# Weight casts in the recurrence hops of a bidirectional RWKV-7 layer: queued behind one kind of copy only

## The chip, the cores and the metric

The kernel runs on one core of a Trainium2 chip. The core has five engines, each with its own queue of instructions, which in the profile it works through in the order of the program: TensorE (PE, with a separate row PEld for its weight loads), VectorE (DVE), ScalarE (ACT), GpSimd (POOL) and SyncE (SP, which here only starts DMA transfers). The metric is the device time of one execution in microseconds, lower is better.

## The reference

The reference computes one layer of a diffusion backbone on 640 tokens: 128 context tokens and 512 latent tokens. Each token goes through a modulated norm and a wide projection; that feeds a bidirectional RWKV-7 recurrence (8 heads of width 64), an attention branch, two sigmoid gates, an output projection and a feed-forward block. All weights are float32. What matters here is the recurrence, run once forward and once backward per head:

```python
def _wkv_step(s, inp):
    r, w, k, v, a, b = inp
    sa = jnp.einsum("bhvk,bhk->bhv", s, a)
    s = s * w[:, :, None, :] + sa[..., None] * b[:, :, None, :] + v[..., None] * k[:, :, None, :]
    return s, jnp.einsum("bhvk,bhk->bhv", s, r)
...
s_f, y_f = _wkv_scan(s0[:, 0], rh, _heads(decay[:, :, 0]), _heads(k_dir[:, :, 0]), vh,
                     -kk, kk * _heads(iclr[:, :, 0]), False)
s_b, y_b = _wkv_scan(s0[:, 1], rh, _heads(decay[:, :, 1]), _heads(k_dir[:, :, 1]), vh,
                     -kk, kk * _heads(iclr[:, :, 1]), True)
...
merged = (jax.nn.sigmoid(gate_rw) * (o_rw @ p["w_o_rwkv"])
          + jax.nn.sigmoid(gate_na) * (o_na @ p["w_o_na"]))
```

## The kernel before

**Products in three parts.** Every float32 matrix is split into a rounded part `hi` and a rest `lo`, and a product is three matmuls: hi by hi, hi by lo, lo by hi. For a weight tile of 128x1024 that lies in `wst`, `wcast` (L184) makes the two parts. In the form that the stretch here mostly uses, ScalarE does two passes over the tile: `wlo = -wst` (L190) and `whi = wst` rounded (L192), and a DMA that POOL starts (L191) adds `wst` into the negated tile. In the other form ScalarE does the pass L192 alone and VectorE subtracts (L195).

**The recurrence in chunks of 64 tokens.** The 8 heads are taken as four pairs, `ct` = 0 to 3. For each pair the program goes through `main` (builds the triangular matrices `Nt` from `AG`, L1189), `inv` (inverts them on VectorE, gives `Rt`), and `carry` (L1371 on), which walks through eight hops `s` = 0 to 7. A hop serves both directions and both heads at once. In the profile a hop is this ring of small operations:

- PE multiplies `AG` by the state `ZV` (L1393), ScalarE copies the result to `x` (L1396). In the list of instructions the tile is `x`, its name in the code is `x0`.
- PE multiplies `Rt` by `x` (L1420), ScalarE copies these products into `ZV` (L1426).
- PE multiplies `TG` by `ZV` (L1433, and L1450 for the output), VectorE multiplies by the decay into the next state in `ZV` (L1445).

The hop after it can't start before L1445. At the end of `carry` ScalarE copies the output out (L1455).

**What fills the ring.** `carry` is a generator that stops three times in each hop: behind the copy to `x`, behind the copies into `ZV`, and behind the decays. At each stop `weave` (L1588) reads one entry of a table `plan` and queues other work: first so many matmuls from `fill` (the large projections, L223), then, by the entry's last digit, preparation of the next head pair through `beside` (L520): digit 1 stands for the second stretch (behind the copies into `ZV`), digit 2 for the third (behind the decays). The first stretch gets fill alone. `beside` queues items until a budget is spent, `bud=((1.8, 0.8), (1.3, 1.8))`: microseconds of ScalarE and of VectorE that the author gave to the second and to the third stretch. Each item states its own cost as such a pair.

**Two sources of items.** `beside` looks first at `pend`, work that the fill left for later (a copy of a finished projection out of PSUM, its token shift `u_out` and `shift` at L545 to L554, its activation L573, the cast of the next weight tile), and takes the head of that list if it is due. Otherwise it takes the next item of the generator `pg`. For `ct` 0 to 2 that is `prep` for the next head pair: norms and LoRA products (L645 to L684), decays (L693 to L707), the keys `NK` (L721 on ScalarE, L723 and L728 on VectorE), the tiles `BK` (L738, L742), `bv` (L747, L751). For `ct` = 3 it is `gate_a`, VectorE's gating of the merged attention output (L1579). What is left of `pg` in hop 7 is drained there by `last` (before the copies into `ZV` for `ct` 0 and 1, behind them for `ct` 2 and 3), and then VectorE makes the next pair's `AG` (L1168), which the next `main` needs. `NK` is a tile with a single buffer: the second direction's `NK` may be written only when L738, L742 and L747 have read the first one.

**The cast's place.** `stream` (L805 on) runs the projections unit by unit and, an eighth into each, leaves the cast of the next unit's weight tile in `pend`, due at once. Inside `carry` (`hold`) an item that is late by less than 24 fill matmuls isn't forced out, so `beside` decides where it goes. PE, POOL, DVE and ACT take this part of the program in exactly the order in which it is written (`manual_schedule(engines=FIRST)`).

## Time and profile before

| what | value |
|---|---|
| median of 3 runs | 1151.08 us (1150.06 to 1152.26) |
| the profiled execution, its own time | 1151.04 us |
| its span in the profile | 1149.3 us |
| TensorE busy in the span | 1117.0 us, 97% |
| ScalarE, VectorE, GpSimd busy | 533.7, 777.8, 195.1 us |
| granted TensorE clock | 0.995 of full speed |
| cast passes L190 and L192 | 1.02 to 1.07 us each for 128x1024 |

The times in the profile are in microseconds from the start of the span. The four `carry` stretches lie at about 298 to 342, 394 to 437, 492 to 536 and 598 to 630 us. In a row of the timeline stand: start, time from the first start to the last end, engine, line, operation, result and operand, shapes, count, and in brackets how long the engine sat idle before and who released it. Matmul rows overlap each other, so a PE row that starts where the row ahead ends is a PE that doesn't wait.

### The profile page before, as it was taken

The page shows a single profiled execution, that of the slowest core. Times are in us where ns is not written, and L with a number is a line of the kernel's source. Part 1 is how long each engine was busy: PE and PEld are TensorE (multiplying, and loading weights), DVE is VectorE, ACT ScalarE, POOL GpSimd, SP SyncE. Part 2 cuts the span into 40 slices and gives each one's busy share as a digit, 9 for nine tenths or more (in the row PEclk, how much of TensorE's full clock was granted, in tenths as well). Part 3 has the DMA queues.
Part 4 walks back from the last instruction along what each step waited for, and adds up shares of the span by engine and source line. Part 5 has one row for each costly group of instructions (what it writes and reads, how often), then busy time and mean ns, then how long its engine had stood idle before and what let it go on. Part 6 is the DMA issues. An engine that isn't in the chain of part 4 may idle for free.

```text
span 1149.3 us, 26860 instructions
## 1 busy us (share of the span) xinstructions
PE 1117.0 (97%) x11160; PEld 990.9 (86%) x11160; DVE 777.8 (68%) x1641; ACT 533.7 (46%) x1052; POOL 195.1 (17%) x262
## 2 busy tenths in 40 slices
PE   6999999999999999999999999999999999999998
PEld 4688878799888888888898788999899989998997
DVE  4565465769558847936787846897478747874775
ACT  4444576665465665456443524654134413441340
POOL 1163244321101212120100421110101010101000
PEclk8999999999999999999999999999999999999999
DMA  9752677654433533343743872222212221232122
GB/s 340 261 113 91 199 277 236 198 153 125 107 75 86 148 85 93 96 119 86 254 122 105 265 213 72 92 93 93 91 56 92 94 90 55 92 97 88 55 91 94
DMA packets 60482, 149.16 MB, mean 130 GB/s; under 512 B 7460, under 2 KB 22436, under 8 KB 60360
## 3 DMA queue, kind: packets, MB, share of 16 engines
q1 hardware_dynamic: 54888, 131.16, 34.7%
q0 software_dynamic: 4032, 14.68, 6.5%
q10 hardware_dynamic: 1440, 1.59, 0.5%
q8 instruction: 88, 1.44, 0.5%
q14 instruction: 34, 0.28, 0.1%
HBM read 118.41 MB, written 14.32 MB: 115 GB/s over the span
## 4 chain that ended last, share of the span: by engine, by line
PE 74%; DVE 10%; issue 8%; ACT 4%; DMA 2%; POOL 1%; SPq 0%; ACTq 0%; DVEq 0%; POOLq 0%
PE acc L311 24%; PE f L1856 21%; PE fl L223 8%; PE mm L223 5%; PE psa L1044 1%; PE lg L959 1%; PE pt L988 1%; DVE RL L1321 1%; DVE pr L1317 1%; PE po L1006 1%; PE w L1420 1%; PE w L1393 1%; DMA o<-o_d 1%; PE w L1433 1%; DMA wlo<-wst 1%
## 5 line engine op out<-in xcount | busy, mean ns | idle before, releaser
L1856 PE MATMUL f<-t,whi 128*128 128x320 f32 x640 | 141.7, 310 | 0.2
L311 PE MATMUL acc<-whi,u 128*128 128x512 f32 (+1 forms) x448 | 136.1, 386 | 0.0
L1856 PE MATMUL f<-b,whi 128*128 128x320 f32 x608 | 135.0, 310 | 0.4 <-DVE b L212 0.4
L223 PE MATMUL fl<-h,whi 128*128 128x320 f32 x672 | 121.4, 321 | 0.0
L1856 PEld LDWEIGHTS f<-t,whi 128*128 128x128 f32 x640 | 106.8, 188 | 0.8 <-issue 0.4
L223 PEld LDWEIGHTS fl<-h,whi 128*128 128x128 f32 x672 | 102.1, 189 | 4.6
L192 ACT CAST whi<-wst 128x1024 fp32r<-128x1024 f32 (+1 forms) x77 | 79.3, 1033 | 52.2 <-PE acc L311 41.5
L1856 PEld LDWEIGHTS f<-b,whi 128*128 128x128 f32 x608 | 101.7, 188 | 1.1 <-issue 0.6
L1856 PE MATMUL f<-t,wlo 128*128 128x320 f32 x320 | 98.9, 309 | 0.0
L311 PEld LDWEIGHTS acc<-whi,u 128*128 128x128 f32 x448 | 83.5, 188 | 16.6
L1856 PE MATMUL f<-b,wlo 128*128 128x320 f32 x304 | 94.1, 309 | 0.0
L1909 ACT CAST whi<-ws 128x1024 fp32r<-128x1024 f32 x40 | 42.0, 1051 | 104.5 <-PE f L1856 45.6
L311 PE MATMUL acc<-wlo,u 128*128 128x512 f32 (+1 forms) x224 | 86.3, 385 | 0.0
L1923 POOL TENSOR_TENSOR ws<-wst 128x512 f32<-128x512 f32 x20 | 29.1, 1454 | 334.7 <-DVE wlo L1912 226.3
L195 DVE TENSOR_TENSOR wlo<-wst,whi 128x1024 fp32r<-128x1024 f32 (+2 forms) x57 | 60.1, 1066 | 30.6 <-ACT whi L192 30.0
L311 PE MATMUL acc<-whi,h 128*128 128x512 f32 x240 | 79.2, 404 | 0.8 <-DVE h L436 0.8
L1724 DVE SCALAR_TENSOR_TENSOR tt<-acc,G 128x512 f32<-128x512 f32 (+1 forms) x51 | 34.7, 680 | 59.0 <-PE acc L311 45.4
L223 PE MATMUL fl<-h,wlo 128*128 128x320 f32 x336 | 63.8, 322 | 0.0
L1909 ACT CAST whi<-wst 128x1024 fp32r<-128x1024 f32 (+1 forms) x48 | 41.3, 869 | 42.3 <-PE acc L311 25.1
L1856 PEld LDWEIGHTS f<-t,wlo 128*128 128x128 f32 x320 | 60.1, 188 | 0.0
L1912 DVE TENSOR_TENSOR wlo<-ws,whi 128x1024 fp32r<-128x1024 f32 x40 | 55.4, 1386 | 5.4 <-ACT whi L1909 5.4
L1445 DVE TENSOR_TENSOR ZV<-w,Dt 64x128 f32<-64x128 f32 x64 | 18.4, 288 | 58.5 <-PE w L1433 57.4
(342 smaller groups left out, 2533.2 us busy)
## 6 DMA issues: line engine op xcount, KB each, us to landing
wst<-in_w_dram SPq DMA_DIRECT2D x66, 512.0 KB
wst<-in_w_rw_dram SPq DMA_DIRECT2D x31, 512.0 KB
wlo<-wst POOLq DMA_DIRECT2D x28, 512.0 KB, 4.7
wa<-in_w_ada_dram SPq DMA_DIRECT2D x24, 512.0 KB
f<-in_w_ada_dram SPq DMA_DIRECT2D x16, 512.0 KB
wst<-in_w_qkv_dram SPq DMA_DIRECT2D x12, 512.0 KB
o<-o_d SPq DMA_DIRECT2D x14, 320.0 KB
x<-in_xs_dram SPq DMA_DIRECT2D x8, 512.0 KB
```

The lines of the kernel that those rows point to most:

```text
L192: act.copy(hi[:, :n], st[:, :n])
L195: dve.tensor_tensor(out=lo[:, a:b], in0=st[:, a:b], in1=hi[:, a:b].bitcast(F32), op=ALU.subtract)
L223: pe.matmul(ps[:, :t1 - t0], w[:, a:a + 128], x[:, k0 + kt, t0:t1], start=n == 0, stop=n == 3 * nk - 1)
L311: pe.matmul(pss[i][:, a:b], lhs(x, kt, ts_), w[:, cs_], start=ki == 0 and n == 0, stop=ki == last and n == 2)
L959: pe.matmul(psl[:, hd, o_:o_ + n], qT[ft][rows, qs], x[rows, :], start=True, stop=True)
L988: pe.transpose(pst[:, c * 128:(c + 1) * 128], L[:, c * 128:(c + 1) * 128], ident)
L1445: dve.tensor_tensor(out=V(ZV[own, l + 1, h, :], [[128 * dl, 2], [1, 64]]), in0=V(pn[own, :], [[64, 2], [1, 64]], 64 * g), in1=V(Dt[own, 0, ...
L1724: dve.scalar_tensor_tensor(out=tt, in0=ps[:, a:b], scalar=c, in1=G[:, g, sl], op0=ALU.mult, op1=ALU.mult)
L1856: pe.matmul(ps[:, :H2], w_[:, c_], x_[:, kt, :], start=first and kt + n == 0, stop=last and kt == 3 and n == 2, skip_group_check=more)
L1909: act.copy(r[0][:, :width], src())
L1912: dve.tensor_tensor(out=r[1][:, :width], in0=src(), in1=r[0][:, :width].bitcast(F32), op=ALU.subtract)
L1923: eng_x(PRM["se"][i - 1]).tensor_tensor(out=o_, in0=x, in1=y, op=op)
```

## The change

Three edits. The cast's stated cost goes from 1.05 to 2.1 us of ScalarE. `beside` no longer takes the head of `pend` but looks through all due items: first those whose ScalarE cost is over 2 (only the casts), and these only if it was called for the second stretch (`wide`); then the others that are due. `weave` says which stretch it is.

```diff
-    def beside(gen, budget):
+    def beside(gen, budget, wide):
...
-            if pend and pend[0][0] <= 0:
-                _, c, fn = pend.pop(0)
+            due = [p for p in pend if p[0] <= 0]
+            due = [p for p in due if p[1][0] > 2 and wide] + [p for p in due if p[1][0] < 2]
+            if due:
+                _, c, fn = due[0]
+                pend[:] = [p for p in pend if p is not due[0]]
                 fn()
...
-                    later(lambda i=i: cast(i + 1), (1.05, 0), -off[0])
+                    later(lambda i=i: cast(i + 1), (2.1, 0), -off[0])
...
-                            beside(o_, bud[n - 1])
+                            beside(o_, bud[n - 1], n == 1)
```

In the second stretch's budget of 1.8 a cast now leaves no room for anything else; before, an item of `prep` followed it. No instruction is added or removed, but many of `prep` move to a later hop. Behind L526 the changed file's lines carry numbers that are 3 higher (L1429 there is L1426 before).

ScalarE, hops 6 and 7 of `ct` = 0, before. `x_682` and `x_688` are the two hops' copies to `x`; `U` and `vp` belong to a projection's token shift, `NK_4332` is the second direction's key tile:

```order
L1396 COPY x_682_4264<-w_4259 128x128
L1426 COPY ZV<-w_4275 64x2x64 x2
L545 COPY U_4057<-fl_4170 128x192
L546 COPY U_4057<-fl_4170 128x128
L551 ACTIVATE vp_627<-U_4057,D 128x128
L551 ACTIVATE vp_627<-U_4057,D 128x512
L190 ACTIVATE wlo_4313<-wst_4168 128x1024
L192 CAST whi_4312<-wst_4168 128x1024
L1396 COPY x_688_4322<-w_4317 128x128
L747 COPY bv_4329<-NK_4203 128x320 x2
L721 ACTIVATE NK_4332<-pre_4066,D 128x320 x2
L1426 COPY ZV<-w_4347 64x2x64 x2
```

The same place on ScalarE in the changed kernel:

```order
L1399 COPY x_681_4262<-w_4257 128x128
L1429 COPY ZV<-w_4273 64x2x64 x2
L190 ACTIVATE wlo_4288<-wst_4147 128x1024
L192 CAST whi_4287<-wst_4147 128x1024
L548 COPY U_4048<-fl_4149 128x192
L549 COPY U_4048<-fl_4149 128x128
L554 ACTIVATE vp_627<-U_4048,D 128x128
L554 ACTIVATE vp_627<-U_4048,D 128x512
L1399 COPY x_687_4320<-w_4315 128x128
L750 COPY bv_4329<-NK_4252 128x320 x2
L724 ACTIVATE NK_4332<-pre_4161,D 128x320 x2
L1429 COPY ZV<-w_4347 64x2x64 x2
```

The cast went from behind the token shift (third stretch) to directly behind hop 6's copies into `ZV`, and the token shift now stands behind it.

VectorE at `ct` = 0 from hop 5's decays on to the next pair's `AG`, before. `f_680` and `f_691` are the two directions' `BK`:

```order
L1445 TENSOR_TENSOR ZV<-w_4213,Dt_2031 64x2x64 x2
L728 TENSOR_TENSOR NK_4203<-NK_4203,kt__626 128x640
L738 SCALAR_TENSOR_TENSOR f_680_4257<-NK_4203,pre_3893 128x10x64
L552 SCALAR_TENSOR_TENSOR vp_627<-U_4057,C,vp_627 128x128
L554 SCALAR_TENSOR_TENSOR vp_627<-U_4057,C,vp_627 128x128
L1445 TENSOR_TENSOR ZV<-w_4266,Dt_2031 64x2x64 x2
L552 SCALAR_TENSOR_TENSOR vp_627<-U_4057,C,vp_627 128x512
L554 SCALAR_TENSOR_TENSOR vp_627<-U_4057,C,vp_627 128x512
L742 TENSOR_TENSOR f_680_4257<-NK_4203,pre_3893 128x10x64
L723 SCALAR_TENSOR_TENSOR NK_4332<-pre_4066,kk_4002 128x640
```

The same place on VectorE in the changed kernel:

```order
L1448 TENSOR_TENSOR ZV<-w_4203,Dt_2031 64x2x64 x2
L726 SCALAR_TENSOR_TENSOR NK_4252<-pre_3949,kk_4033 128x640
L731 TENSOR_TENSOR NK_4252<-NK_4252,kt__626 128x640
L1448 TENSOR_TENSOR ZV<-w_4264,Dt_2031 64x2x64 x2
L555 SCALAR_TENSOR_TENSOR vp_627<-U_4048,C,vp_627 128x128
L557 SCALAR_TENSOR_TENSOR vp_627<-U_4048,C,vp_627 128x128
L555 SCALAR_TENSOR_TENSOR vp_627<-U_4048,C,vp_627 128x512
L557 SCALAR_TENSOR_TENSOR vp_627<-U_4048,C,vp_627 128x512
L741 SCALAR_TENSOR_TENSOR f_688_4326<-NK_4252,pre_3948 128x10x64
L745 TENSOR_TENSOR f_688_4326<-NK_4252,pre_3948 128x10x64
L726 SCALAR_TENSOR_TENSOR NK_4332<-pre_4161,kk_4033 128x640
```

Three of these moved behind hop 6's decays: the two short token-shift passes and the first direction's L738 (now L741). From L723 of the second direction on to L1168 the order is the same in both.

VectorE in hop 5 of `ct` = 3, before. `mx_8653` gates a finished projection that lies in the PSUM tile `fl_8734`:

```order
L1579 SCALAR_TENSOR_TENSOR kk_8283<-pre_8655,kk_8283 128x320 x2
L1579 SCALAR_TENSOR_TENSOR bv_8420<-pre_8689,bv_8420 128x320 x2
L1554 SCALAR_TENSOR_TENSOR mx_8653<-mx_8653,fl_8734 128x320
L1556 TENSOR_TENSOR mt_7932<-mt_7932,mx_8653 128x320
L1445 TENSOR_TENSOR ZV<-w_8771,Dt_6879 64x2x64 x2
L195 TENSOR_TENSOR wlo_8813<-wst_8626,whi_8812 128x768
```

The same place in the changed kernel, where that tile is called `fl_8736`:

```order
L1582 SCALAR_TENSOR_TENSOR bv_8420<-pre_8659,bv_8420 128x320 x2
L195 TENSOR_TENSOR wlo_8794<-wst_8630,whi_8793 128x768
L1448 TENSOR_TENSOR ZV<-w_8771,Dt_6879 64x2x64 x2
L1557 SCALAR_TENSOR_TENSOR mx_8657<-mx_8657,fl_8736 128x320
L1559 TENSOR_TENSOR mt_7932<-mt_7932,mx_8657 128x320
```

The cast's VectorE half (L195) moved from behind hop 5's decays to ahead of them, and the gating that reads the PSUM tile moved from ahead of them to behind. In hop 2 of `ct` = 3, L195 stands directly ahead of the decays too.

## The prediction, made before the changed kernel ran

> **What bounds the kernel.** I read the page's first part, then the table of stretches, then the waits, then the timeline where the two orders differ. Page first:

> ```profile
> span 1149.3 us, 26860 instructions
> PE 1117.0 (97%) x11160; PEld 990.9 (86%) x11160; DVE 777.8 (68%) x1641; ACT 533.7 (46%) x1052; POOL 195.1 (17%) x262
> ```

> PE is busy for all but 32 us of the span: whatever makes it wait adds to the time, and little can be won. The table of stretches for the four `carry` stages (columns: start:end, us, then busy us and count of PE, PEld, DVE, ACT, POOL, the granted clock, the DMA share, GB/s):

> ```profile
> 298.00:342.00 44.00, 42.35 (x596) 36.61 (x595) 16.98 (x35) 27.50 (x71) 6.12 (x10) 1.00 0.33 82
> 394.00:437.00 43.00, 41.47 (x591) 35.91 (x591) 21.01 (x41) 26.62 (x71) 6.83 (x9) 1.00 0.31 85
> 492.00:536.00 44.00, 42.88 (x602) 37.55 (x602) 18.11 (x37) 26.62 (x72) 5.91 (x9) 1.00 0.37 98
> 598.00:636.00 38.00, 37.96 (x570) 32.81 (x570) 24.42 (x56) 13.52 (x40) 0.51 (x1) 1.00 0.41 125
> ```

> PE idles 1.65, 1.53, 1.12 and 0.04 us there, 4.3 us together: the ceiling of any gain. What ScalarE's queue costs PE at the copy to `x`, from the view of line L1396 ("who waited for it"), in all 32 hops:

> ```profile
>   PE w L1420: 1.6, 5
> ```

> So 1.6 us is what a cast, or something else ahead of that copy, costs now. The other side is what the cast pushes back.

> **The change, `ct` = 0.** The cast of hop 6 moves ahead of the token shift, `prep` runs one item or two later. The timeline of hops 6 and 7:

> ```profile
> 335.01 0.32 ACT L545 COPY U<-fl 128x192 f32<-128x192 f32 x1
> ...
> 335.53 1.02 ACT L551 ACTIVATE vp<-U,D 128x128 f32<-128x128 f32 x2
> ...
> 336.04 0.35 DVE L552 SCALAR_TENSOR_TENSOR vp<-U,C,vp 128x128 f32<-128x128 f32 x1 [1.94 <-ACT vp L551]
> ...
> 336.45 1.04 ACT L190 ACTIVATE wlo<-wst 128x1024 fp32r<-128x1024 f32 x1
> ...
> 337.40 1.03 ACT L192 CAST whi<-wst 128x1024 fp32r<-128x1024 f32 x1
> 337.54 0.75 DVE L552 SCALAR_TENSOR_TENSOR vp<-U,C,vp 128x512 f32<-128x512 f32 x1
> ...
> 338.99 0.82 DVE L742 TENSOR_TENSOR f<-NK,pre 128x640 f32<-128x640 f32 x1
> ...
> 341.31 0.73 PE L1450 MATMUL w<-TG,ZV 128*64 128x64 f32 x8 [0.71 <-ACT ZV L1426]
> ...
> 344.09 3.36 DVE L1168 TENSOR_TENSOR AG<-kk,P 64x640 f32<-64x640 f32 x4
> ...
> 347.50 1.27 PEld L1189 LDWEIGHTS w<-AG,f 64*32 64x32 f32 x122 [0.21 <-DVE AG L1168]
> ```

> The last row is what decides: the next `main` (L1189) waited for `AG`, so VectorE's tail of `prep` is already the end of the chain, with no slack. In the changed order that tail is longer. The two passes take 336.45 to 338.43, 1.98 us, and now lie ahead of L545, so the token shift's first VectorE pass starts 1.98 us after 336.04, at 338.0. Four shift passes follow (0.85 us from 336.04 to hop 6's decays at 336.89, and 1.45 us from 337.54 to 338.99): 340.3. Then L738 and L742, which both stand there now, 0.82 us each: 341.95. From the end of L742 to the end of L1168 the order is as before, 339.81 to 347.45, 7.64 us: `AG` is ready at 349.6 instead of 347.45, 2.1 us later. On the way, hop 7's copies into `ZV` stand behind L721, which needs L742, so PE waits the same 2 us already at L1450; both are one delay. I take 2.1. Up to hop 6 I count nothing, though hop 0 changes:

> ```profile
> 303.73 1.23 DVE L1445 TENSOR_TENSOR ZV<-w,Dt 64x128 f32<-64x128 f32 x4 [6.01 <-PE w L1433]
> ...
> 304.56 1.28 PE L664 MATMUL w<-K,pre 128*128 128x2 f32 x10 [0.42 <-ACT pre L660]
> ```

> L664 and six LoRA matmuls covered hop 0's decays there and move to hop 1; PE now goes on at 304.56, then waits for the decays until 305.0. These 0.4 us are got back where LoRA matmuls that stood ahead of a hop now stand behind it. Bounds: 0 if the tail had cover, 2.8 if hops 0 to 5 lose 0.7.

> **`ct` = 1.** The tail again, and VectorE beside POOL:

> ```profile
> 432.00 0.61 DVE L1445 TENSOR_TENSOR ZV<-w,Dt 64x128 f32<-64x128 f32 x2 [1.89 <-PE w L1433]
> ...
> 432.64 0.83 DVE L728 TENSOR_TENSOR NK<-NK,kt__626 128x640 f32<-128x640 f32 x1
> ...
> 433.55 2.08 POOL L751 TENSOR_TENSOR bv<-bv,NK 128x640 f32<-128x640 f32 x1 [12.07 <-DVE NK L728]
> ...
> 434.12 2.20 DVE L742 TENSOR_TENSOR f<-NK,pre 128x640 f32<-128x640 f32 x1
> ...
> 438.41 3.37 DVE L1168 TENSOR_TENSOR AG<-kk,P 64x640 f32<-64x640 f32 x4
> ...
> 441.83 1.27 PEld L1189 LDWEIGHTS w<-AG,f 64*32 64x32 f32 x122 [0.22 <-DVE AG L1168]
> ```

> Before, only the second direction's L728, L738, L742 were left behind hop 6's decays; in the changed order all of the first direction's come first: three passes (2.25 us at 0.82 with a little overlap), then ScalarE's L721, 1.2 us, which must wait for L742 because of the single `NK` buffer (its row stands with `ct` = 2). That is 3.45 us ahead of 9.14 us that stay the same (432.64 to 441.78). Against it PE reaches hop 6 earlier by the waits that go:

> ```profile
> PE w L1420 <- ACT x L1396: 0.4, 1, 0.4
> PE w L664 <- ACT pre L660: 0.2, 1, 0.2
> ```

> 0.6 us together. Sum: 2.8 us. L742 is charged at its 2.20 us of this place, though the same pass took 0.82 in `ct` = 0: the POOL row covers it, and POOL's pass stays beside it. At 0.82, from 434.12 only L552's wait for the shift would be left, and the 9.14 shrink to some 7.8: then 1.4 us. Bounds 0.8 and 3.5.

> [...]

> **`ct` = 2.** Here PE arrives a little after `AG`, so a part is hidden:

> ```profile
> 525.62 1.19 ACT L721 ACTIVATE NK<-pre,D 128x320 f32<-128x320 f32 x2
> ...
> 526.83 0.27 ACT L1396 COPY x<-w 128x128 f32<-128x128 f32 x1
> ...
> 529.39 0.61 DVE L1445 TENSOR_TENSOR ZV<-w,Dt 64x128 f32<-64x128 f32 x2 [1.00 <-PE w L1433]
> ...
> 533.57 0.83 DVE L728 TENSOR_TENSOR NK<-NK,kt__626 128x640 f32<-128x640 f32 x1 [1.78 <-ACT NK L721]
> ...
> 538.69 3.37 DVE L1168 TENSOR_TENSOR AG<-kk,P 64x640 f32<-64x640 f32 x4
> ...
> 542.70 1.66 PEld L1189 LDWEIGHTS w<-AG,f 64*32 64x32 f32 x160 [0.44 <-issue]
> ```

> The cast that stood behind hop 4's decays now stands behind hop 5's copies into `ZV` and pushes L705 to L721 up against hop 6's copy to `x`: that copy comes some 0.7 us later, so hop 6's decays end at 530.7 instead of 530.0. Three passes of the first direction follow (533.0); L747 and L721 on ScalarE stand behind hop 7's copies, L721 ends near 535.0 where L728 began at 533.57. 8.5 us stay from there (533.57 to 542.06): 543.6. PE would be there at about 542.9, was at 542.70, so the cost is 0.9 us, taken as 1.0. Bounds 0 and 1.8.

> **`ct` = 3.** PE never idles there, and the decays carry the order:

> ```profile
> 608.99 0.96 DVE L195 TENSOR_TENSOR wlo<-wst,whi 128x768 fp32r<-128x768 f32 x1 [0.89 <-ACT whi L192]
> ...
> 609.67 0.54 ACT L1426 COPY ZV<-w 64x128 f32<-64x128 f32 x2 [0.55 <-PE w L1420]
> ...
> 612.03 0.45 PE L1393 MATMUL w<-ZV,AG 128*64 128x64 f32 x8
> ...
> 620.93 0.49 DVE L1554 SCALAR_TENSOR_TENSOR mx<-mx,fl 128x320 f32<-128x320 f32 x1
> ...
> 621.40 0.83 ACT L192 CAST whi<-wst 128x768 fp32r<-128x768 f32 x1
> ...
> 622.80 0.46 PE L223 MATMUL fl<-o,whi 128*128 128x320 f32 x2
> ```

> Hop 2: the cast now starts behind the copies into `ZV` that end at 610.2; L192 takes 0.83, L195 0.96, the decays 0.61 behind it: 612.7, where PE needed them at 612.03. Cost 0.7. Hop 5: with that 0.7, copies end at 622.1, L192 at 622.9, L195 at 623.9, the decays at 624.5, and only then L1554, to 625.05, which before ran at 620.93. It reads the PSUM tile that PE's fill writes next but one (two `fl` buffers); that fill began at 622.80, now could at 623.5, and waits for 625.1. Cost 1.6, and it covers the wait for the decays. Sum 2.3. Bounds 0.7 (one place only) and 3.

> **Edits that cost nothing.** Python's search through `pend` isn't on the chip. POOL's casting DMA and SP's loads of the next tile follow the cast; a tile is cast 42 fill matmuls ahead of its unit, and a cast moves by at most one hop, so those matmuls cover it.

> **Sum.** 2.1 + 2.8 + 1.0 + 2.3 = 8.2 us on the profiled execution's 1151.04, which is 0.04 below the median: 1159.2. The bounds together are 1.5 and 11.1, but not all four at once.

> **Rivals.**
> - *A gain.* The copies to `x` come free (1.6 us) and VectorE's tail still meets `AG`. For it: ScalarE is busy 27 of 44 us in a stage, so `prep` could catch up. Against it: `prep`'s tail waited for at L1189 with 0.2 us, no slack. It decides if `prep` finishes hop 6 as far as before. Time: 1151.04 - 1.6 = 1149.4.
> - *Half of it.* Only the `ct` = 0 and 1 tails bind, or one of them and `ct` = 3: PE's 34 fill matmuls ahead of L1189 would have to absorb more than they do now. Time: 3 to 5 us, 1155.
> - *Nothing happens.* What PE waits for in one hop it would have waited for in another, all inside the ring's slack: 1151. Against it: the sums of two tails end past their user.

> **How the numbers follow.** A measurement of this kernel tells about 0.2%, 2.3 us, from no change. The forecast (5.5 to 11) gets 0.75, half of it 0.12, a gain 0.08, nothing 0.05. A gain of 1.6 is inside 0.2%, and only 0.04 of its 0.08 goes beyond with part of the 4.3 us. Slower 0.87, same 0.09, faster 0.04. The range goes from 1153.5, half of it with one term missing, to 1162.5, the forecast with the higher bounds of the first two; it leaves out the gain and nothing, and some of either end.

> **What would show it.** In the profile after: L1189 of `ct` = 0 waits for L1168 some 2 us later in its stage, with L1450 of hop 7 waiting about 2.5 us for L1426; `ct` = 1 likewise, L742 there again above 2 us; in `ct` = 3 a PE wait of about 1.6 us of L223 on L1554, and about 0.7 of L1393 on L1445. PE's busy time stays at 1117, its idle time grows from 32 to 40 us. I am wrong if the row of L1189 shows no later `AG`: then VectorE had room that I have not seen, most likely because POOL's pass in `ct` = 1 no longer falls on L742.

## The result and the profile after

The changed kernel takes 1161.04 us, the median of 6 runs (1158.88 to 1163.80), against 1151.43 us of the kernel before in the same comparison: 1.0085 times as long, with a 95% interval of 1.0069 to 1.0101. It is 9.6 us slower by the medians. The profiled execution took 1158.88 us, the shortest of the six, and is 7.8 us above that of before. Both differences matter below, since the two are not the same.

From here on lines carry the numbers of the kernel that is shown: the prediction's L1189, L1450, L1426 and L1168 are L1192, L1453, L1429 and L1171 in the changed kernel. The page's first part:

```profile
span 1157.1 us, 26864 instructions
PE 1117.6 (97%) x11160; PEld 990.5 (86%) x11160; DVE 778.2 (67%) x1641; ACT 534.8 (46%) x1052; POOL 196.0 (17%) x262
```

Each engine has as many instructions as before; the four more in the total stand in none of these counts. PE works as long as before (1117.6 us against 1117.0) and idles 39.5 us instead of 32.3. The waits of PE in the recurrence, 296 to 644 us (columns: total, times, longest):

```profile
PE w L1453 <- ACT ZV L1429: 4.5, 2, 2.5
PE w L1423 <- ACT x L1399: 2.5, 5, 0.8
PE w L1192 <- DVE AG L1171: 1.6, 3, 0.6
...
PE fl L223 <- DVE mx L1557: 1.5, 1, 1.5
```

The wait at hop 7's copies into `ZV` was 0.7 us once and is 4.5 us in two hops. The wait at the copies to `x`, which the change should have shortened, grew from 1.6 to 2.5 us. Two waits are new in size: for `AG`, and of a fill matmul for a gate pass. The end of `ct` = 0 in the timeline:

```profile
334.52 1.03 ACT L192 CAST whi<-wst 128x1024 fp32r<-128x1024 f32 x1
...
335.57 0.32 ACT L548 COPY U<-fl 128x192 f32<-128x192 f32 x1
...
336.60 0.35 DVE L555 SCALAR_TENSOR_TENSOR vp<-U,C,vp 128x128 f32<-128x128 f32 x1 [1.40 <-ACT vp L554]
...
340.42 1.20 ACT L724 ACTIVATE NK<-pre,D 128x320 f32<-128x320 f32 x2 [2.44 <-DVE f L745]
...
341.82 0.73 PE L1453 MATMUL w<-TG,ZV 128*64 128x64 f32 x8 [2.54 <-ACT ZV L1429]
...
344.60 3.36 DVE L1171 TENSOR_TENSOR AG<-kk,P 64x640 f32<-64x640 f32 x4
```

It reads in order of time: the second pass of the cast ends at 335.55, and only then the copy to `U` runs; the token shift follows it; L724 waits 2.44 us for L745; PE waits 2.54 us for the copies queued behind L724. The cast is one queue place earlier for ScalarE, and a whole chain of three engines is later.

Two rows of the table of stretches, the first of the kernel before, the second of the changed kernel, show something that neither diff nor order tells. The third number from the end is the granted clock:

```profile
294.00:298.40 4.40, 4.40 (x53) 4.31 (x44) 3.58 (x9) 1.68 (x4) 0.71 (x1) 0.61 0.45 157
```

```profile
342.00:346.60 4.60, 4.60 (x25) 4.44 (x25) 4.54 (x7) 1.07 (x3) 0.00 (x0) 0.63 0.35 136
```

In either execution PE ran at half its clock for 3.4 us (by single microseconds the clock is 0.50, with parts of one at both ends). I count that as 1.7 us lost, half of the 3.4, an estimate that is used below too. The same 18 fill matmuls ahead of hop 0 of `ct` = 0 took 4.38 us with the stretch (before, 294.48 to 298.86) and 2.84 us at full clock (changed kernel, 293.14 to 295.98), 1.54 us more. In the kernel before the stretch lies ahead of the recurrence, behind a pause of 1.25 us at L1359 for which the profile names no releaser and which the changed kernel's execution does not have; in the changed kernel it lies right behind the wait at L1453. So in this execution PE of the kernel before reaches hop 0 of `ct` = 0 (its first matmul, L1393) 2.88 us later than the changed kernel, which waits there for `Rt` and has 1.73 us of that left at L1436. Counted from L1436 of hop 0 in `ct` = 0, which was 1.73 us earlier in the changed kernel, to the last hop of `ct` = 3, which was 7.85 us later, the recurrence takes 9.58 us more. That this equals the difference of the medians, 9.6 us, is partly luck, since it is one execution of each kernel.

The rows of the other stages, `ct` = 1, then 2 and 3:

```profile
438.67 2.06 POOL L754 TENSOR_TENSOR bv<-bv,NK 128x640 f32<-128x640 f32 x1 [13.41 <-DVE NK L731]
...
439.24 2.18 DVE L745 TENSOR_TENSOR f<-NK,pre 128x640 f32<-128x640 f32 x1
439.34 0.59 PEld L1453 LDWEIGHTS w<-TG,ZV 128*64 128x64 f32 x8 [2.26 <-ACT ZV L1429]
...
443.51 3.36 DVE L1171 TENSOR_TENSOR AG<-kk,P 64x640 f32<-64x640 f32 x4
...
446.08 0.30 PE L1192 MATMUL w<-AG,f 64*32 64x64 f32 x2 [0.55 <-DVE AG L1171]
```

```profile
548.45 1.77 PE L1192 MATMUL w<-AG,f 64*32 64x64 f32 x154 [0.50 <-DVE AG L1171]
...
617.81 0.63 PEld L1396 LDWEIGHTS w<-ZV,AG 128*64 128x64 f32 x8 [0.48 <-DVE ZV L1448]
...
630.55 0.56 PE L223 MATMUL fl<-o,whi 128*128 128x320 f32 x2 [1.48 <-DVE mx L1557]
```

`ct` = 1 and 2 end with PE waiting for `AG`; in `ct` = 3 PE waits for the decays in hop 2 and for the gate pass L1557 behind hop 5.

### The profile page after: what moved, and what is told of

Same layout as the page of the kernel before. It is cut to its first block, busy times and chain, and to the rows that moved or that the text cites. A ratio compares the mean times of both kernels' runs of the same rounds, so it can differ in the third digit from the quotient of the medians.

```text
span 1157.1 us, 26864 instructions
## 1 busy us (share of the span) xinstructions
PE 1117.6 (97%) x11160; PEld 990.5 (86%) x11160; DVE 778.2 (67%) x1641; ACT 534.8 (46%) x1052; POOL 196.0 (17%) x262
## 3 DMA queue, kind: packets, MB, share of 16 engines
q10 hardware_dynamic: 1440, 1.59, 0.5%
## 4 chain that ended last, share of the span: by engine, by line
PE 73%; DVE 9%; issue 8%; DMA 4%; ACT 4%; POOL 1%; SPq 0%; DVEq 0%; ACTq 0%; POOLq 0%
PE acc L311 23%; PE f L1859 23%; PE fl L223 8%; PE mm L223 5%; DMA wa<-in_w_ada_dram 3%; PE psa L1047 1%; PE lg L962 1%; PE pt L991 1%; DVE RL L1324 1%; DVE pr L1320 1%; PE po L1009 1%; DMA win<-in_rpbp_dram 1%; PE w L1423 1%; DVE Rt L1356 1%; PE w L1436 1%
## 5 line engine op out<-in xcount | busy, mean ns | idle before, releaser
L223 PE MATMUL fl<-h,whi 128*128 128x320 f32 x672 | 122.1, 322 | 0.0
L223 PEld LDWEIGHTS fl<-h,whi 128*128 128x128 f32 x672 | 102.6, 190 | 4.6
L192 ACT CAST whi<-wst 128x1024 fp32r<-128x1024 f32 (+1 forms) x77 | 79.3, 1032 | 55.9 <-PE acc L311 28.0
L195 DVE TENSOR_TENSOR wlo<-wst,whi 128x1024 fp32r<-128x1024 f32 (+2 forms) x57 | 60.2, 1066 | 34.5 <-ACT whi L192 34.0
L223 PE MATMUL fl<-h,wlo 128*128 128x320 f32 x336 | 63.0, 319 | 0.0
L1859 PEld LDWEIGHTS f<-b,wlo 128*128 128x128 f32 x304 | 57.1, 188 | 0.1
```

The lines of the kernel that those rows point to most:

```text
L192: act.copy(hi[:, :n], st[:, :n])
L195: dve.tensor_tensor(out=lo[:, a:b], in0=st[:, a:b], in1=hi[:, a:b].bitcast(F32), op=ALU.subtract)
L223: pe.matmul(ps[:, :t1 - t0], w[:, a:a + 128], x[:, k0 + kt, t0:t1], start=n == 0, stop=n == 3 * nk - 1)
L1859: pe.matmul(ps[:, :H2], w_[:, c_], x_[:, kt, :], start=first and kt + n == 0, stop=last and kt == 3 and n == 2, skip_group_check=more)
```

## The experiments

Each run was set beside runs of the kernel before on the same chip. The table gives the ratio of the medians with its 95% interval, and what the stages lost in the profiled execution: the time by which PE's same instruction is later than in the profile of before, as growth from L1436 of hop 0 in `ct` = 0 to L1396 of hop 0 in `ct` = 1, from there to L1396 of hop 0 in `ct` = 2, and so on to L1396 of the last hop. "Half clock" counts the stretches of 3.4 us at clock 0.50 within these stages; the kernel before has none there in its profile. "Clock" is the mean granted clock over all runs of the kernel. The stages and the stretches come from one execution of each kernel, the medians from all; the clock of single runs of one kernel differs by up to 0.007 (E7: 0.988 to 0.995), so the stages of a row need not add up to its median.

| kernel | median, us | ratio (95%) | `ct` 0 | 1 | 2 | 3 | half clock | clock |
|---|---|---|---|---|---|---|---|---|
| before | 1151.4 to 1152.0, in E12 1149.8 | 1 | 0 | 0 | 0 | 0 | 0 | 0.9975 to 0.998 |
| changed | 1161.04 | 1.0085 (1.0069 to 1.0101) | 3.5 | 3.0 | 0.8 | 2.3 | 1 | 0.9957 |
| E1 place only | 1157.47 | 1.0052 (1.0039 to 1.0066) | 2.4 | 0.3 | 2.5 | 3.0 | 1 | 0.9965 |
| E2 charge only | 1155.95 | 1.0040 (1.0026 to 1.0055) | 0.8 | 3.8 | 0.0 | 0.0 | 0 | 0.9980 |
| E3 not in `ct` = 3 | 1159.04 | 1.0070 (1.0057 to 1.0084) | 3.2 | 2.5 | 3.7 | 0.0 | 3 | 0.9960 |
| E4 only in `ct` = 3 | 1152.70 | 1.0007 (0.9996 to 1.0017) | -0.2 | 0.0 | -0.1 | 3.8 | 1 | 0.9974 |
| E5 cast last | 1158.57 | 1.0063 (1.0041 to 1.0084) | 3.9 | 2.8 | 0.8 | 0.6 | 1 | 0.9962 |
| E6 no side effects | 1155.08 | 1.0030 (1.0018 to 1.0043) | 4.4 | -0.2 | 0.6 | 0.0 | 2 | 0.9962 |
| E7 `last` behind | 1164.40 | 1.0117 (1.0094 to 1.0140) | 2.7 | 4.2 | 1.0 | 2.3 | 2 | 0.9913 |
| E8 larger budget | 1159.45 | 1.0074 (1.0051 to 1.0097) | 1.9 | 1.0 | 4.0 | 3.0 | 2 | 0.9948 |
| E11 no POOL pass | 1162.03 | 1.0089 (1.0075 to 1.0104) | 3.2 | 2.5 | 2.4 | 3.8 | 2 | 0.9958 |
| E12 no wait behind | 1160.13 | 1.0083 (1.0069 to 1.0097) | 4.6 | 0.5 | 0.8 | 0.0 | 1 | 0.9952 |

### E1 and E2: the place and the charge apart

The change has two halves: where a cast may stand, and what it is charged. E1 keeps the place and gives back the charge:

```
-            due = [p for p in due if p[1][0] > 2 and wide] + [p for p in due if p[1][0] < 2]
+            due = [p for p in due if p[1][0] == 1.05 and wide] + [p for p in due if p[1][0] != 1.05]
...
-                    later(lambda i=i: cast(i + 1), (2.1, 0), -off[0])
+                    later(lambda i=i: cast(i + 1), (1.05, 0), -off[0])
```

> The rule on the place is kept (a cast only in the second stretch of a hop), but the cast is charged 1.05 us again instead of 2.1. In ct = 0 to 2 VectorE's order is then that of the kernel before, although ScalarE's two passes stand where the changed kernel has them; in ct = 3 VectorE's decays stand late as in the changed kernel, and in one hop one gate pass later still. Theory (the tails of ct = 0 to 2 come from prep items pushed back by the charge, ct = 3 from the place): only the term of ct = 3 is left, 2.3 us on the median of 1151.4, so 1153.7, up to 1155.5 with the gate pass; L1192 of ct = 0 and 1 waits as little for AG as before (0.2 us). Rival (the passes at the copies into ZV delay the hop itself, whatever prep does): about 1160.

E2 keeps the charge and gives back the place (the head of `pend` alone is looked at):

```
-            due = [p for p in due if p[1][0] > 2 and wide] + [p for p in due if p[1][0] < 2]
+            due = [p for p in due[:1] if p is pend[0]]
```

> The other half: the cast is charged 2.1 us, but may stand in any stretch, as before. VectorE's order in ct = 2 and 3 is that of the kernel before; in ct = 0 and 1 prep's passes move behind decays as in the changed kernel. Theory: the terms of ct = 0 and 1 alone, 2.1 + 2.8 us on 1151.4: 1156.3, and no wait of L223 on the gate pass in ct = 3. Rival (the place decides): 1151.4.

E2 came out near what theory said, 4.0 us slower for 4.9, with nothing lost in `ct` = 2 and 3; but `ct` = 0 lost 0.8 us where 2.1 was expected, and `ct` = 1 lost 3.8 where 2.8 was. E1 did not: 1157.5, above theory's 1155.5 and below the rival's 1160. `ct` = 1 is free of loss there, `ct` = 3 loses its term, but `ct` = 0 loses 2.4 us although no item of `prep` was pushed back. Its rows:

```profile
336.23 0.35 DVE L555 SCALAR_TENSOR_TENSOR vp<-U,C,vp 128x128 f32<-128x128 f32 x1 [3.96 <-ACT vp L554]
...
337.42 0.77 PE L1396 MATMUL w<-ZV,AG 128*64 128x64 f32 x8 [2.09 <-DVE ZV L1448]
```

VectorE sits idle for 3.96 us until the shift's activation behind the two passes is done, and the decays of hop 6 stand behind the shift. So my joint theory falls: the place alone (the cast ahead of the shift) makes a loss in `ct` = 0, of which 1.7 us are put down to a half-clock stretch behind that wait, and the loss of `ct` = 1 comes from the charge. E1's path is not quite that of the changed kernel, where hop 6's decays stand ahead of the shift and its lateness shows at L724 and L1453. In `ct` = 2 a part of E1's 2.5 us is another wait: PE waited 1.50 us for a load of `o` that costs 0.3 us in the kernel before. E3 and E8 show the same wait (1.69 and 1.36 us); in E9 to E11 it is 0.9 to 1.2 us, in the other profiles at most 0.7. As E9 and E10 have the order of the kernel before, the change need not be behind it. What makes that load late was not traced.

### E3 and E4: the last stage and the first three

A flag keeps the old rule and the old charge in the stages not named (E4 has `ct == 3` in its place):

```
+            due = [p for p in due if p[1][0] > 2 and wide] + [p for p in due if p[1][0] < 2] if new[0] else [p for p in due[:1] if p is pend[0]]
...
-                hold[0] = True
+                hold[0], new[0] = True, ct < 3
```

> The changed rule and charge in ct = 0 to 2, the old ones in ct = 3. Theory: the changed kernel's 1161.0 less the 2.3 us of ct = 3: 1158.7; the wait of 1.5 us of L223 on the gate pass in ct = 3 is gone, the waits of ct = 0 and 1 at L1453 and L1192 stay. Rival (stages hand their lateness on to one another, so that ct = 3 only shows what came earlier): 1161, or the same loss at another place of ct = 3.

> The opposite: the changed rule and charge in ct = 3 alone. Theory: 2.3 us on 1151.4: 1153.7, with L223 waiting about 1.5 us for the gate pass at hop 5 and 0.7 us at hop 2. Rival (as with the changed rule in ct = 0 to 2 alone): no loss of its own, 1151.4. If the stages add up, this run and the one without ct = 3 together lose what the changed kernel loses, 9.6 us between the medians.

E3 is at 1159.0 where 1158.7 was expected, and its last stage loses nothing. E4's trace shows the wait of the changed kernel (1.48 us there):

```profile
622.44 0.57 PE L223 MATMUL fl<-o,whi 128*128 128x320 f32 x2 [1.47 <-DVE mx L1557]
```

with a half-clock stretch behind it, at 624 us; without the 1.7 us put down to that stretch the stage lost 2.1 us. By the medians E4 lost only 0.8 us, with an interval of -0.5 to +2.0, so 2.3 lies just outside it, while the changed kernel less E3 gives 2.5 us. Together E3 and E4 lose 7.9 us by the medians, not 9.6. The mechanism and its place are shown; its size is 2.3 us in the trace of the changed kernel, and between 0.8 and 2.5 by times.

### E5, E6: the cast without its side effects

E5 turns the order among the due entries round, so that the copy to `U` and the shift go ahead of the cast:

```
-            due = [p for p in due if p[1][0] > 2 and wide] + [p for p in due if p[1][0] < 2]
+            due = [p for p in due if p[1][0] < 2] + [p for p in due if p[1][0] > 2 and wide]
```

> As the changed kernel (second stretch only, 2.1 us), but the cast comes last among the entries that are due, not first. The copies to U and the token shift of ct = 0 then stand ahead of the two passes again. After the first runs (place alone: hop 7 of ct = 0 starts 2 us late behind VectorE's decays; charge alone: the tail of ct = 0 loses only 0.5 us) theory says that the tail of ct = 0 is late because of the shift behind the passes: 1.6 us less than the changed kernel's 1161.0, so 1159.4, and L1171 of ct = 0 starts as in the run with the charge alone, about 0.5 us late relative to hop 6. The wait of about 2.5 us at L1453 of ct = 0 falls to about 1.4. Rival (prep's pushed-back passes make the tail, wherever the shift stands): 1161, wait unchanged.

E6 has the same order, but charges 1.05 us and has the old rule in `ct` = 3; VectorE's order is then that of before throughout.

> The place alone, without what comes with it: second stretch only, but the cast last among the due entries, charged 1.05 us, and the old rule in ct = 3. VectorE's order is that of the kernel before from the first to the last instruction; on ScalarE five casts stand elsewhere than before, each at most one hop later. Theory: no term of the loss is left, and of the waits at the copies to x those behind a cast go (0.4 us in ct = 1): 1151 to 1151.9, not to be told from before. Rival (two passes behind the copies into ZV cost the hop something in every stage): 1155 or more. Other rival (the change is a gain once prep keeps its place): 1150 or less.

E5's time fits the expectation, 1158.6 for 1159.4, but not for its reason. Two rows of E5, then the wait and the table row of E6:

```profile
342.69 0.89 PE L1453 MATMUL w<-TG,ZV 128*64 128x64 f32 x8 [3.61 <-ACT ZV L1429]
...
343.58 3.37 DVE L1171 TENSOR_TENSOR AG<-kk,P 64x640 f32<-64x640 f32 x4
```

```profile
341.98 0.98 PE L1453 MATMUL w<-TG,ZV 128*64 128x64 f32 x8 [2.87 <-ACT ZV L1429]
```

```profile
341.00:348.00 7.00, 6.02 (x27) 5.90 (x28) 6.70 (x9) 2.21 (x5) 0.85 (x1) 0.51 0.65 167
```

`AG` starts as theory said (343.58, where before has 344.09 and a hop 6 that is 1.24 us later: 0.7 us late in its stage, 0.5 expected). But the cast now finds no room in hop 6 and lands in hop 7 ahead of the copies into `ZV`. PE waits 3.61 us there instead of the 1.4 expected, and this time PE, not VectorE, is last at L1192. In `ct` = 3 the same turn saves 1.7 of the 2.3 us. E6 lost 3.1 us with VectorE's order untouched: the expectation of no loss falls, and all of its loss stands in `ct` = 0, a wait of 2.87 us and 6.8 us at half clock behind it. At each of the other places tried for this cast in hops 6 and 7 of `ct` = 0 that stage lost time (2.4 us in E1, 3.9 in E5, 4.4 in E6); none was found as good as the one that it had before, behind the shift's activations and ahead of hop 7's copy to `x`.

### E7 and E12: nothing behind the cast that PE waits for

E7 is the changed kernel with the rest of `prep` queued behind the copies into `ZV` of hop 7 in all four stages:

```
-    lh=(0, 0, 1, 1)
+    lh=(1, 1, 1, 1)
```

> The changed kernel, but in ct = 0 and 1 the rest of prep of hop 7 is queued behind the copies into ZV instead of ahead of them, as it already is in ct = 2 and 3. L1453 of hop 7 then no longer waits for copies behind L724; its waits of 2.5 and 2.0 us go. Theory (they and the wait for AG at L1192 are one delay): PE reaches L1192 earlier and waits there for AG instead; the time stays within 1 us of 1161.0. Rival (two delays): 4.5 us less, 1156.5.

The wait at L1453 is gone, and PE waits for `AG` instead, as this row of its waits says:

```profile
PE w L1192 <- DVE AG L1171: 6.9, 9, 2.4
```

`AG` starts at 347.37, in a stage whose hop 6 is 2.77 us later than that of the changed kernel: 344.60 plus 2.77, to the hundredth the same place. That is what theory called one delay, and the rival's 1156.5 is far off. But the time did not stay within 1 us of 1161.0, as theory said: 1164.4, 12.4 us above the kernel before, where the changed kernel is 9.6. Its profile idles no more (39.2 us against 39.5); its mean clock is the lowest so far, 0.9913. PE now pauses in several pieces, up to 2.4 us, and half-clock stretches follow in both stages.

E12 is E6 with this setting:

> The run without the side effects, and in addition the rest of prep (and with it the cast that had come to stand ahead of hop 7's copies into ZV in ct = 0) is queued behind these copies in ct = 0 and 1. VectorE's order is still that of the kernel before. Theory (the 3.1 us that this placement cost came from the wait of 2.9 us at L1453 of ct = 0 and the half-clock stretch that followed it): L1453 waits 0, L1192 for AG at most 1 us longer, and the median is 1151 to 1152.5. With the waits for x that are gone it could be 1150, below both kernels, but hardly to be told from before. Rival (the passes cost ScalarE's queue something elsewhere too): 1154 or more.

That expectation failed clearly: 1160.1, 10.4 us above the kernel before. The wait at L1453 is gone as expected and L1192 starts 2.5 us ahead of before, but then:

```profile
353.68 0.51 PE L1262 MATMUL w<-K,f 64*64 64x64 f32 x19 [3.09 <-issue]
```

PE stood 3.09 us for something that the profile does not name (0.42 us at this place before), with 3.4 us of half clock behind it. Later, outside the recurrence, PE waited 3.2 us for a weight tile's DMA (0.6 us before), with 6.8 us of half clock. The transfers of the cast and of the next tile run together at this moment (DMA share, in steps of 2 us, 0.93 to 1.09 from 344 to 350 us, 0.22 to 0.74 before). That they delay what L1262 needs is argued, not shown: in the kernel before the share is 1.00 to 1.12 from 349 to 351 us, just ahead of the same place, and PE waits 0.42 us there. The cause stays open.

### E8: a budget that fits the charge

```
-    bud=((1.8, 0.8), (1.3, 1.8))
+    bud=((2.9, 0.8), (1.3, 1.8))
```

> The changed kernel with the second stretch's ScalarE budget raised from 1.8 to 2.9 us, so that a prep item still follows a cast charged 2.1; in ct = 0 to 2 prep's passes then stand as early as before or earlier. Theory (the charge pushes prep back in hops 0 to 6 of ct = 0 and in the tail of ct = 1): those 1.4 and 3 us go, the shift behind the passes in ct = 0 (up to 2) and ct = 3 (2.3) stay: 1151.4 + 4.3 = 1155.7. Rival (more work behind the copies into ZV makes every hop's next copy to x late): 1160 or more, with the waits of L1423 for x grown from 2.5 to above 5 us.

The part that theory spoke of came: `ct` = 1 loses 1.0 instead of 3.0 us. The time did not: 1159.5. `ct` = 0 waits 2.09 us at L1396 for the decays behind the shift, as in E1; `ct` = 2 loses 4.0 us, 1.7 of it put down to half clock and about 1 in the load of `o`; and `ct` = 3 loses 3.0 us. The rival's growing waits for `x` did not come either (1.3 us).

### E9 and E10: what a pause of PE costs

The half-clock stretches stand behind pauses of PE in most of these profiles. To measure that alone, the kernel before got pauses at 8 fixed places (E10 with 4 in the place of 10):

```
-                act.copy(x0[:, :ng, :], V(px[:, :], [[64, ng], [1, 64]]))
+                for _ in range(1 + 10 * (s in (2, 5))):
+                    act.copy(x0[:, :ng, :], V(px[:, :], [[64, ng], [1, 64]]))
```

> The kernel before, with ScalarE's copy to x written eleven times over instead of once in hops 2 and 5 of each ct (same values): PE pauses there 8 times, for about 10 x 0.27 = 2.7 us less what it has of cover, some 2.4 us. It leaves nothing out. Theory (a pause of 2 us or more at these places is often followed by 3.4 us at half the granted clock, 1.7 us lost each, as behind the wait of 2.5 us at L1453 in the changed kernel): clock rows of 0.5 behind some of the 8 pauses, mean granted clock at or below 0.993 against 0.9975 before, and 1151.9 + 19 + at least 5 = 1176 or more. Rival (the half-clock stretches come at random and have nothing to do with pauses): mean clock 0.997 and 1151.9 + 19 = 1171 or less.

> The same with five copies instead of one: 8 pauses of about 4 x 0.27 = 1.1 us less the cover, some 0.8 us. Theory (short pauses are seldom followed by half clock): mean clock 0.997 as before, 1151.9 + 6.5 = 1158.5. Rival (any pause is followed by it): mean clock as low as with the long pauses, 1164 or more. With the long pauses this gives the price of a pause: its own length, or its length and 1.7 us.

The kernel before took 1151.47 us beside them. E10: 1160.26, ratio 1.0078 (1.0063 to 1.0093), mean clock 0.9978. E9: 1186.46, ratio 1.0299 (1.0282 to 1.0317), mean clock 0.986, 0.983 to 0.990 in single runs. The waits at the copies to `x`, first of E9, then of E10:

```profile
PE w L1421 <- ACT x L1397: 23.9, 11, 3.3
```

```profile
PE w L1421 <- ACT x L1397: 9.6, 11, 1.5
```

Before, they were 1.6 us. E10's 8.0 us more of waiting cost 8.8 us. E9's 22.3 us more cost 35.0 us, and the 12.7 us that are left are about what the clock lost: 0.9977 less 0.986, times 1184, is 13.8 us. One of E9's pauses and the two stretches around it:

```profile
334.01 0.45 PE L1421 MATMUL w<-x,Rt 64*64 64x64 f32 x8 [2.96 <-ACT x L1397]
```

```profile
330.00:334.00 4.00, 1.04 (x25) 0.84 (x24) 0.26 (x1) 3.64 (x13) 0.00 (x0) 1.00 0.28 108
334.00:338.00 4.00, 3.99 (x33) 3.48 (x34) 0.45 (x2) 0.52 (x2) 0.00 (x0) 0.57 0.00 0
```

Theory holds against both rivals: pauses of about 1 us cost about their own length, pauses near 2.7 us cost 1.6 times as much (35.0 for 22.3).

### E11: VectorE beside POOL

```
-    kb="ddpd"
+    kb="dddd"
```

> The changed kernel with the sum L754 of ct = 1 on VectorE instead of POOL, as in ct = 0, so that no POOL pass stands beside L745. Theory (L745's 2.18 us come from the POOL pass beside it): L745 takes 0.82 us, L754 adds 0.82 us on VectorE, so L1171 starts 0.5 us earlier in its stage, and the time is 0.5 us under the changed kernel's 1161.0, less than can be told. Rival (L745 is long for another reason there): 2.18 us stays and VectorE's tail is 0.8 us longer.

```profile
439.37 0.82 DVE L745 TENSOR_TENSOR f<-NK,pre 128x640 f32<-128x640 f32 x1
440.11 0.82 DVE L754 TENSOR_TENSOR bv<-bv,NK 128x640 f32<-128x640 f32 x1
...
443.02 3.37 DVE L1171 TENSOR_TENSOR AG<-kk,P 64x640 f32<-64x640 f32 x4
```

L745 takes 0.82 us once POOL's pass is gone, and `AG` starts 0.5 us earlier than in the changed kernel (in stages that begin 0.14 us apart). The time, 1162.0, does not tell the two apart, as expected. In the changed kernel L745 started 0.57 us behind the start of POOL's pass and ended 0.69 us behind its end (441.42 and 440.73 us); 2.18 us beside that pass and 0.82 us without it are the price here.

## Why the prediction was right, and where it was not

Forecast: 1159.2, range 1153.5 to 1162.5. Measured: 1161.04. The sign, the stages and their mechanisms were those named; the sum was short by 1.4 us against the difference of medians. That the range holds the result is in part luck: the reason given for its upper end, the forecast with the higher bounds of the first two terms, makes 8.2 + 0.7 + 0.7 = 9.6 us and 1160.6, not 1162.5, and even all four upper bounds make only 1162.1.

- **`ct` = 0, predicted 2.1, measured 3.5.** What the shift's lateness does was right to a tenth: from hop 6, where PE was 1.45 us ahead of before, to `ct` = 1, where it was 1.78 us behind, are 3.2 us; 1.2 of these are PE running at half clock behind the pause (PE reached L1192 at 349.19, `AG` was ready at about 348.0, since L1189 started 3.41 us after L1168 did before), and 2.0 remain. Hops 0 to 6 cost 0.3 us, where I took 0 with a bound of 0.7. L1453 waited 2.54 us, as said (2.5). What was missing is the price that this pause has on top of its length; with it the stage lies above its upper bound of 2.8. PE was also later than `AG`, so the row of L1192 shows no wait for `AG` there, though `AG` came 2.0 us late in its stage. The sign of being wrong that I had named, no later `AG` in that row, would have misled here. E5, E6 and E7 show how little the name in the row means: PE came to L1192 3.1 us behind the end of `AG` in E5 and 4.1 in E6, and 2.5 us ahead of it in E7.
- **The reason for `ct` = 0.** I gave both the shift behind the passes and items of `prep` pushed back. E1 shows that the first alone is enough for a loss of 2.4 us, E2 that the second alone is worth 0.8 us.
- **`ct` = 1, predicted 2.8, measured 3.0.** L745 took 2.18 us beside POOL, as taken. E2 alone loses 3.8 us and E1 0.3: it is the charge.
- **`ct` = 2, predicted 1.0, measured 0.8.** Neither half makes it alone in the recurrence's hops (E2 0.0; E1's 2.5 us are mostly elsewhere).
- **`ct` = 3, predicted 2.3 (0.7 and 1.6), measured 2.3:** 0.6 us up to hop 3 and 1.7 behind hop 5, with the waits at the two places named. E3 takes it away entirely, E4 shows it in a stage by itself.
- **The copies to `x`.** I counted on 0.6 us gained in `ct` = 1, 0.4 of it at a copy to `x`, and no more. All in all the waits there grew from 1.6 to 2.5 us: the copy of hop 7 in `ct` = 0 now stands behind the late shift's activations (0.8 us), and hop 2 of `ct` = 0 and of `ct` = 2 wait 0.5 and 0.6 us where they didn't before.
- **Idle time** went from 32.3 to 39.5 us (forecast 40), with PE's busy time unchanged.
- **The sum.** 3.5 + 3.0 + 0.8 + 2.3 = 9.6 us. The term that was mis-sized is that of `ct` = 0, by the half clock behind the pause at L1453. The mean clock says the same of all runs: 0.9957 against 0.9975 is 0.0018 times 1160, 2.1 us, a part of it at places where PE would have waited anyway. The two profiled executions differ by only 7.8 us because that of before has a pause and a half-clock stretch of its own ahead of the recurrence.

None of the variants is faster than the kernel before; the nearest, E4, can't be told from it.

## What to carry to other kernels

Moving work to a "free" place in one engine's queue has to be costed by what stands behind it there and on the engines that wait for that: here 2 us on ScalarE, off the critical path by its busy share, came back through a token shift, VectorE's passes behind it and TensorE. A planner's charge is part of the order: making a cost truer without refitting the budget delays whatever comes next. And on a TensorE that is 97% busy, count a pause near 2.7 us at more than its length: here 8 pauses of about 2.7 us cost 35.0 us, 8 of about 1 us cost 8.8.

## What the runs showed of the hardware

That half clock follows pauses of 1.25 to 3.6 us, though not all of them, was not expected. From 100 us on to the last few microseconds of these profiles the granted clock is 1.00 or, for stretches of 3.4 us (6.8 us in E6, and once in E12), 0.50. Behind each of the six pauses of 2.5 us and more at L1453 and L1262 (2.54 us in the changed kernel, 2.55 in E3, 3.61 in E5, 2.87 in E6, 2.6 in E11, 3.09 in E12) such a stretch began within about 2 us of the pause's end, in E3 and E6 already ahead of it. Of E9's eight pauses (2.7 to 3.3 us) six were followed by one in its profiled execution, two were not; of pauses of 1.2 to 2.1 us some were (2.09 us in E1 and E8, 1.99 us in E3, 1.25 us in the kernel before) and others not (1.99 us in the changed kernel, in E2 and E5; 1.6 us at L590 in every profile). E9, where nothing but copies on ScalarE was added, shows by its mean clock of 0.986, against 0.9978 with four copies in the place of ten, that the pauses are the cause and not a companion.

```profile
310.57:313.99 3.42, 2.38 (x35) 2.00 (x33) 2.34 (x5) 1.56 (x7) 0.00 (x0) 1.00 0.07 21
313.99:317.40 3.41, 1.72 (x16) 1.48 (x16) 0.83 (x1) 2.66 (x10) 0.00 (x0) 1.00 0.00 0
...
331.05:334.47 3.42, 0.46 (x9) 0.40 (x9) 0.00 (x0) 2.62 (x10) 0.00 (x0) 1.00 0.04 16
334.47:337.88 3.41, 3.41 (x25) 2.96 (x25) 0.33 (x2) 0.52 (x2) 0.00 (x0) 0.50 0.00 0
```

The first pause, 2.73 us, is split into 1.0 and 1.7 us; the second, 2.96 us, falls into one step nearly whole. PE idled 2.0 to 3.0 us in the step ahead of each of E9's six stretches, 2.26 us ahead of that of the changed kernel at 342.97, 2.55 us ahead of E11's at 342.82, and 1.85 and 2.41 us ahead of E12's at 355.24 and 686.33. In the profiles of the kernel before and of the changed kernel, from 100 to 1140 us, none of the 599 full-clock steps with less than 1.2 us of idling was followed by a step at half clock. Of the steps between 1.2 and 1.8 us, those with 1.25 us (kernel before, at 291.20) and 1.47 us (E11, at 629.53) were followed by one; those with 1.69 us (E9, above) and 1.59 us (changed kernel, at 551.19) were not. The pause of 1.99 us was followed by half clock in E3, where one step held 1.79 us of idling, and not in the changed kernel, where it held 1.20. The two stretches of 6.8 us are those where PE idled another 0.93 and 0.80 us within the first half-clock step. What decides between 1.2 and 1.8 us stays open.
